# Layer 0's network: staged key weights scaled and stored behind the latest silu on ScalarE

## The chip, the core and the metric

The kernel runs on one core of one Trainium2 chip. The metric is the device time of one execution in microseconds (us). The core has five instruction queues that run side by side and wait for each other by semaphores: TensorE (PE in the profile; its weight loads are PEld), VectorE (DVE), ScalarE (ACT), GpSimd (POOL) and SyncE (SP), which computes nothing and issues most of the transfers. ACT and POOL issue some transfers as well. Each queue runs its instructions in the order in which they were put into it.

## The reference

The program is a two-layer decoder trunk for 512 tokens of width 1024. Layer 0 is a Mamba-2 mixer followed by a gated network with a width-3 causal convolution; layer 1 is differential attention, whose keys and values come from the stream after layer 0, followed by the same kind of network. What the change touches is the network of layer 0 and the key weights:

```python
def conv_ffn(x, ln_g, up_w, conv_w, conv_b, down_w):
    u = causal_dwconv(rms_norm(x, ln_g) @ up_w, conv_w, conv_b)
    gate, up = u[..., :FFN_DIM], u[..., FFN_DIM:]
    return (jax.nn.silu(gate) * up) @ down_w

def shared_kv(x, kv_ln_g, kv_w, k_norm_g):
    kv = rms_norm(x, kv_ln_g) @ kv_w          # first half of kv_w: the key weights
```

FFN_DIM is 2816, that is 22 blocks of 128 features. The gain `kv_ln_g` can be multiplied into the rows of `kv_w` ahead of time, and the kernel does so for the key half (1024x1024): it loads it, scales it row by row, and stores the scaled copy in a scratch tensor `ks` in DRAM, from which attention loads it later.

## The kernel before

Every product is made of three: each operand is split into a high part (rounded by an ACT copy) and a low part (the rest, by a DVE subtraction). For weights that means, for each chunk of 128x1024: a load on SP into a `wr_...` tile (three buffers), an ACT copy into `wh_...`, a DVE subtraction into `wl_...` (three buffers each), and then PE. `chunk()` lets ACT and DVE prepare two chunks ahead of the one that PE is about to use; a buffer comes free when PE is done with the chunk three places earlier.

PE's order is written out by hand in layer 0's network (`tc.manual_schedule`); on ACT, DVE and SP a scheduler sets the order from what the program issues, from its dependences and from its own estimate of when each will be ready. `with tc.issue_after(ins):` adds an order: what the block issues on the engine of `ins` stands behind `ins` there.

The network takes the 22 blocks in three parts (0 to 5, 6 to 13, 14 to 21). A plain block ("P") is two chunks, `h0_p_0` for the gate and `h0_p_1` for the up side. Blocks 8, 9 and 12, 13 are done in pairs ("S") by seven smaller products, in the order 5, 1, 2, 6, 7, 3, 4, with chunks `U0m_p`; plain chunks are mixed in between them. After its products, each block goes through the convolution (`taps`: one ACT copy at L1066, two DVE steps at L1068), the silu of the gate (L1478 for plain blocks, L1208 for pairs), the product of the two sides (L1160 on DVE), and a split into `sh`, `sl` (L1083 on ACT, L1084 on DVE), from which the down products take their input.

The staging is a side job in the same loop. `stage()` is called after each step and alternates: on one call `key_weights_in` loads an eighth of the key weights (512 KB) into the tile `stage` on SP (L1005), two calls later `key_weights_out` scales its two halves on ACT (L1011) and stores them to `ks`, issued from ACT too (L1012). There is one buffer: the load of the next eighth waits on SP until the store of this one has landed, and the scalings wait on ACT until the load has landed. Eight such rounds are made. The scheduler is free in where it puts them on ACT and SP, since nothing in layer 0 reads `ks`.

Of the kernel before, what the change touches and what calls it, by code (L numbers as in the profile page):

```python
# [12 lines left out]
AF = mybir.ActivationFunctionType  # L13
# [32 lines left out]
def trunk_kernel(ctx: ExitStack, tc, x, ssm_ln_g, ssm_in_w, ssm_conv_w, ssm_conv_b, ssm_dt_bias,  # L46
# [4 lines left out]
    act, dve, pool, pe, sync = nc.scalar, nc.vector, nc.gpsimd, nc.tensor, nc.sync  # L51
# [105 lines left out]
    state = {"next": 0, "use": 0, "hooks": {}}  # L157
# [842 lines left out]
    def key_weights(k0, i):  # L1000
        return ks[k0 * P:(k0 + 2) * P, i * 512:(i + 1) * 512].rearrange("(k p) c -> p k c", p=P)

    def key_weights_in(pl, n):
        v = pl.tile([P, 1024], F32, tag="stage", name="stage%d" % n, bufs=1).rearrange("p (k c) -> p k c", k=2)
        sync.dma_start(v, w_cols(kv_w, n // 2 * 2, 2, n % 2 * 512, 512)[0])  # L1005
        return n, v

    def key_weights_out(n, v):
        k0, i = n // 2 * 2, n % 2
        for k in range(2):  # L1010
            act.activation(v[:, k], v[:, k], AF.Copy, scale=c2[:, 32 + k0 + k:33 + k0 + k])  # L1011
        act.dma_start(key_weights(k0, i), v)  # L1012
# [19 lines left out]
    def ffn(l, norm, bp, gnext, nnext):  # L1032
        with (tc.tile_pool(name="ffn_h%d" % l, bufs=1) as hp, tc.tile_pool(name="ffn%d" % l, bufs=1) as fp,
# [23 lines left out]
            def taps(j, p, u):  # L1057
                key = "%s%d_%d" % ("gu"[j], l, p)
                if j:
                    v = bp.tile([P, T], F32, tag="nsq", name="v" + key, bufs=2)  # L1060
                elif l and vs[0] % 4 > 1:
                    v = bp.tile([P, T], F32, tag=("nacc", "nr")[vs[0] % 2], name="v" + key)
                else:
                    v = fp.tile([P, T], F32, tag="v", name="v" + key, bufs=2 if l else 4)
                vs[0] += 1 - j
                act.activation(v, u, AF.Identity, bias=tap_col(j, p, 3), scale=tap_col(j, p, 2))  # L1066
                for s in range(1, 3):
                    dve.scalar_tensor_tensor(out=v[:, s:], in0=u[:, :T - s], scalar=tap_col(j, p, 2 - s),  # L1068
                                             in1=v[:, s:], op0=ALU.mult, op1=ALU.add)
                return v  # L1070
# [404 lines left out]

            def tapped(p, us):
                ga = taps(0, p, us[0])
                act.activation(ga, ga, AF.Silu)  # L1478
                return ga, taps(1, p, us[1])

            staged = {"n": 0, "at": 0, "v": None}

            def stage():

                staged["at"] += 1
                if staged["v"] and staged["at"] > 1:
                    key_weights_out(*staged["v"])
                    staged.update(v=None, at=0)
                elif not staged["v"] and staged["n"] < KB and staged["at"] > 1:
                    staged.update(v=key_weights_in(fp, staged["n"]), n=staged["n"] + 1, at=0)  # L1490

            def plain(p, sides):

                pss = []
                for _ in whole(p, pss):
                    yield
                sides["open"] = p, tapped(p, pss)

            def gate(sides):
                p, (ga, up) = sides.pop("open")  # L1500
                gated(p, ga, up, sides)
                return ga
# [20 lines left out]
            for q in quarters[:2]:  # L1523
                split_whole(*q)
            gated(0, *tapped(0, (u0[:, 0], u0[:, 1])), sides)
            for q in quarters[2:]:
                split_whole(*q)
            u1 = evac(1, ps1)
            sums = chain(x_sums(0, *tmp[:2]), x_sums(2, *tmp[2:]))
            for p in range(2, 6):  # L1530
                for _ in plain(p, sides):
                    if p > 2:
                        next(sums, None)
                if p == 2:
                    gated(1, *tapped(1, (u1[:, 0], u1[:, 1])), sides)
                ga = gate(sides)
                next(sums, None)
                if p == 3:
                    down_ahead(*parts[0], "z")
                if not l and p == 3:  # L1540
                    bias_ranges(u_tile("ranges"), ga)
# [15 lines left out]
            for i in range(1, len(parts)):  # L1557
# [23 lines left out]
                for kind, p, step in order:  # L1581
                    if kind == "D":
                        q0, m = parts[i - 1]
                        down(q0, m, [behind[q0 + 2 * j] for j in range(m // 2)], False)
                        gate(sides)
                        continue
                    if p not in gens:
                        gens[p] = (plain if kind == "P" else double)(p, sides)
                    next(gens[p])
                    if kind == "P" and step == 1:  # L1590
                        run(gens[p])
                        if p > p0:
                            gate(sides)
                    if not l:
                        stage()
# [454 lines left out]
```

## Time and profile before

| what | value |
|---|---|
| median of 3 runs | 1314.4 us (1312.15 to 1316.61) |
| profiled execution, its own time | 1314.86 us |
| its span, first to last instruction | 1313.2 us |
| TensorE's mean granted clock | 0.999 |
| PE busy | 1304.0 us, 99% of the span |
| DVE, ACT, POOL busy | 1074.7, 748.0, 184.8 us |
| layer 0's network on PE | about 377 to 730 us of the span |
| scalings of staged key weights, L1011 | 16, first 360.6, last 433.2 us |

The span is read in microseconds from the first instruction. PE is almost always busy, so what counts is where it is not: the waits of PE, and stretches in which the granted clock (PEclk) is under 1.00. The busy shares of the other engines matter only where PE waits for one of them. A row of the timeline gives the start, the duration, the engine, the line, the operation with its output and inputs, and in brackets the idle time before it with what ended it.

### The profile page before, as it was taken

Reading aid. Unit: us, or ns where it says so; the run is one execution under the profiler, and the core shown is the slowest. Engines: PE = TensorE matmul, PEld = TensorE weight load, DVE = VectorE, ACT = ScalarE, POOL = GpSimd, SP = SyncE. Lnnn points to the kernel's source line nnn. Section 1 sums busy time; section 2 is a strip of 40 time slices with the busy share of each in tenths; the row PEclk is TensorE's granted clock in tenths of the full one; section 3 lists DMA queues with packets and bytes.
Section 4 is the critical chain, followed back from the end, with each engine's and each line's share of the span. In section 5 each row is a group of like instructions: output and inputs, shape, how many; then the busy total and the mean of one; then the engine's idle time right before and its main releaser. Section 6 shows DMA issues by size and latency. Waiting matters only on the chain.

```text
span 1313.2 us, 18936 instructions
## 1 busy us (share of the span) xinstructions
PE 1304.0 (99%) x7059; PEld 1106.4 (84%) x7059; DVE 1074.7 (82%) x1796; ACT 748.0 (57%) x1234; POOL 184.8 (14%) x212
## 2 busy tenths in 40 slices
PE   9999999999999999999999999999999999999998
PEld 8878888888888798999889887877888889988887
DVE  7989878889879876986768878677789977997776
ACT  6696554743367545653445667777656535643442
POOL 5230200300020421020002310000020030020001
PEclk9999999999999999999999999999999999999999
DMA  7553533432366797769337663222233586566325
GB/s 210 154 154 91 151 99 102 145 98 75 105 191 183 182 219 156 154 144 212 101 88 144 175 146 112 81 65 65 63 107 89 145 204 156 141 123 187 99 62 128
DMA packets 198588, 174.18 MB, mean 133 GB/s; under 512 B 7964, under 2 KB 172192, under 8 KB 198496
## 3 DMA queue, kind: packets, MB, share of 16 engines
q1 hardware_dynamic: 164336, 119.69, 30.9%
q0 software_dynamic: 30704, 47.99, 19.0%
q10 hardware_dynamic: 3456, 5.30, 1.2%
q8 instruction: 55, 0.90, 0.3%
q14 instruction: 37, 0.30, 0.1%
HBM read 166.51 MB, written 6.44 MB: 132 GB/s over the span
## 4 chain that ended last, share of the span: by engine, by line
PE 94%; DVE 2%; ACT 2%; DMA 1%; issue 0%; DVEq 0%; ACTq 0%; SPq 0%
PE ps_in L246 5%; PE ps_in L248 5%; PE ps_in L247 5%; PE ps_g L248 4%; PE ps_g L246 4%; PE ps_g L247 4%; PE ps_u L246 4%; PE ps_u L247 4%; PE ps_u L248 4%; PE ps_s L1439 3%; PE ps_s L1444 3%; PE ps_s L1442 3%; PE ps_s L1338 3%; PE ps_s L1341 3%; PE ps_s L1343 3%; PE ps_o L247 2%
## 5 line engine op out<-in xcount | busy, mean ns | idle before, releaser
L246 PE MATMUL ps_in<-xgh,wh_in 128*128 128x512 f32 x304 | 122.9, 404 | 0.0
L196 DVE TENSOR_TENSOR wl_h<-wr_h,wh_h 128x1024 fp32r<-128x1024 f32 x72 | 88.4, 1231 | 40.7 <-ACT wh_h L185 38.1
L248 PE MATMUL ps_in<-xgh,wl_in 128*128 128x512 f32 x304 | 119.7, 394 | 0.0
L247 PE MATMUL ps_in<-xgl,wh_in 128*128 128x512 f32 x304 | 119.2, 392 | 0.0
L248 PE MATMUL ps_g<-xgh,wl_h 128*128 128x512 f32 x288 | 112.9, 392 | 2.2 <-DVE wl_h L196 2.2
L247 PE MATMUL ps_g<-xgl,wh_h 128*128 128x512 f32 x288 | 112.7, 391 | 0.4 <-DVE xgl L1084 0.4
L246 PE MATMUL ps_g<-xgh,wh_h 128*128 128x512 f32 x288 | 113.0, 392 | 0.0
L246 PE MATMUL ps_u<-xgh,wh_h 128*128 128x512 f32 x288 | 112.1, 389 | 0.0
L247 PE MATMUL ps_u<-xgl,wh_h 128*128 128x512 f32 x288 | 112.1, 389 | 0.0
L248 PE MATMUL ps_u<-xgh,wl_h 128*128 128x512 f32 x288 | 112.1, 389 | 0.0
L185 ACT ACTIVATE wh_h<-wr_h 128x1024 fp32r<-128x1024 f32 x72 | 76.2, 1059 | 59.7 <-PE ps_u L247 17.2
L1083 ACT ACTIVATE sh<-vg 128x512 fp32r<-128x512 f32 (+1 forms) x81 | 42.2, 530 | 60.1 <-DVE vg L1160 35.1
L1238 POOL DMA_DIRECT2D wz<-in_ffn_down_w_dram x28 | 33.8, 1229 | 285.9 <-DVE wl_s L1277 125.2
L248 PEld LDWEIGHTS ps_in<-xgh,wl_in 128*128 128x128 f32 x304 | 57.1, 188 | 12.2 <-issue 0.4
L246 PEld LDWEIGHTS ps_in<-xgh,wh_in 128*128 128x128 f32 x304 | 57.2, 188 | 11.6 <-issue 1.3
L247 PEld LDWEIGHTS ps_in<-xgl,wh_in 128*128 128x128 f32 x304 | 57.3, 188 | 11.0 <-issue 0.5
L248 PEld LDWEIGHTS ps_g<-xgh,wl_h 128*128 128x128 f32 x288 | 54.5, 189 | 14.1 <-DVE wl_h L196 2.6
L247 PEld LDWEIGHTS ps_g<-xgl,wh_h 128*128 128x128 f32 x288 | 54.4, 189 | 11.8 <-DVE xgl L1084 0.8
L1444 PE MATMUL ps_s<-sl,wh_s 128*128 128x256 f32 x252 | 64.1, 283 | 0.0
L1442 PE MATMUL ps_s<-sh,wh_s 128*128 128x256 f32 x252 | 64.1, 283 | 0.0
L185 ACT ACTIVATE wh_in<-wr_in 128x1024 fp32r<-128x1024 f32 x39 | 41.2, 1057 | 39.8 <-PE ps_in L247 30.0
L1276 ACT ACTIVATE wh_s<-wz 128x1024 fp32r<-128x1024 f32 (+2 forms) x38 | 37.3, 981 | 46.7 <-PE ps_s L1343 16.5
(512 smaller groups left out, 3795.4 us busy)
## 6 DMA issues: line engine op xcount, KB each, us to landing
wr_h<-in_ffn_up_w_dram SPq DMA_DIRECT2D x60, 512.0 KB, 4.3
wr_in<-in_ssm_in_w_dram SPq DMA_DIRECT2D x40, 512.0 KB, 3.9
wz<-in_ffn_down_w_dram POOLq DMA_DIRECT2D x21, 512.0 KB, 5.8
m<-cumd POOLq DMA_DIRECT2D x16, 512.0 KB, 4.4
wr_out<-in_ssm_out_w_dram SPq DMA_DIRECT2D x16, 512.0 KB, 3.5
wr_s<-in_ffn_down_w_dram SPq DMA_DIRECT2D x13, 512.0 KB, 4.3
wr_h<-in_ffn_up_w_dram SPq DMA_DIRECT2D x24, 256.0 KB, 3.5
wx<-in_ffn_down_w_dram POOLq DMA_DIRECT2D x12, 512.0 KB, 7.2
```

The source lines that it names most:

```text
L185: return act.activation(self.wh[:, :self.n], self.raw[:, :self.n], AF.Copy)
L196: return eng.tensor_tensor(out=self.wl[:, :self.n], in0=self.raw[:, :self.n], in1=self.wh[:, :self.n].bitcast(F32), op=ALU.subtract)
L246: pe.matmul(ps, wh, xh, start=start, stop=False)
L247: pe.matmul(ps, wh, xl, start=False, stop=False)
L248: return pe.matmul(ps, wl, xh, start=False, stop=stop).ins
L1083: act.activation(hi, v, AF.Copy)
L1338: pe.matmul(pss[b], h, ws[q][1][:, cols], start=False, stop=end and q == qs[-1], skip_group_check=more)
L1341: pe.matmul(pss[b], h, ws[q][0][:, cols], start=first and q == qs[0], stop=False, skip_group_check=more)
L1343: pe.matmul(pss[b], w, ws[q][0][:, cols], start=False, stop=False, skip_group_check=more)
L1439: pe.matmul(v[:, b], wl[:, q, cols], h, start=False, stop=q == nq - 1, skip_group_check=not opens or b > 0)
L1442: pe.matmul(v[:, b], wh[:, q, cols], h, start=opens and q + b == 0, stop=False, skip_group_check=not opens or b > 0)
L1444: pe.matmul(v[:, b], wh[:, q, cols], w, start=False, stop=False, skip_group_check=not opens or b > 0)
```

## The change

The reference to the last silu instruction of a plain block is kept in `state["silu"]`, and the scalings and the store of a staged eighth are issued inside `tc.issue_after(state["silu"])`, that is, on ACT they stand behind the latest silu that the program has issued by then. The loads (L1005, on SP) have no such order of their own, nor has the last call after the loop. Nothing is added to or taken from the work.

```diff
             def tapped(p, us):
                 ga = taps(0, p, us[0])
-                act.activation(ga, ga, AF.Silu)
+                state["silu"] = act.activation(ga, ga, AF.Silu).ins
                 return ga, taps(1, p, us[1])
...
                 staged["at"] += 1
                 if staged["v"] and staged["at"] > 1:
-                    key_weights_out(*staged["v"])
+                    with tc.issue_after(state["silu"]):
+                        key_weights_out(*staged["v"])
                     staged.update(v=None, at=0)
```

The order of PE's and POOL's instructions is the same before and after. On ACT, DVE and SP it moves. In the names below the number at the end is that of the tile; the eight staged eighths are stage_4323, 4833, 4976, 5142, 5296, 5463, 6060 and 6225.

The first place is ACT where block 3 ends and blocks 4 and 5 begin, near 428 us of the profile. `vg_3` is the gate of block 3, `vg_4` that of block 4, `sh_3959` the split of blocks 2 and 3. Before:

```order
L185 ACTIVATE wh_h_5_1_4120<-wr_h_5_1_4118 128x1024
L1066 ACTIVATE vg_4_4150<-ps_g_4_4084,cf_90 128x512
L1011 ACTIVATE stage_6225<-stage_6225,c_89 128x512 x2
L1478 ACTIVATE vg_3_4034<-vg_3_4034 128x512
L1012 DMA ks<-stage_6225 128x2x512
L1083 ACTIVATE sh_3959<-vg_3_4034 128x512
```

With the change:

```order
L185 ACTIVATE wh_h_5_1_4120<-wr_h_5_1_4118 128x1024
L1066 ACTIVATE vg_4_4150<-ps_g_4_4084,cf_90 128x512
L1478 ACTIVATE vg_3_4034<-vg_3_4034 128x512
L1083 ACTIVATE sh_3959<-vg_3_4034 128x512
L185 ACTIVATE wh_h_6_0_4173<-wr_h_6_0_4171 128x1024
```

The eighth round, and with it all sixteen scalings, are gone from this part; the silu of block 3 no longer stands behind them.

The second place is ACT between the pairs 8, 9 and 12, 13, near 525 to 535 us of the profile. `u_8` holds the products of blocks 8 and 9, `wh_U_12_5054` and `wh_U_12_5113` are the high parts of the first two chunks of the pair 12, 13. Before:

```order
L185 ACTIVATE wh_h_11_0_5012<-wr_h_11_0_5010 128x1024
L1083 ACTIVATE sh_4969<-vg_10_4959 128x256
L1152 ACTIVATE wh_U_12_5054<-wz_0_3669 128x1024
L1066 ACTIVATE vg_8_5041<-u_8_4763,cf_90 128x512
L1083 ACTIVATE sh_4969<-vg_10_4959 128x256
L1066 ACTIVATE vg_9_5045<-u_8_4763,cf_90 128x512
```

With the change:

```order
L185 ACTIVATE wh_h_11_0_5012<-wr_h_11_0_5010 128x1024
L1011 ACTIVATE stage_5142<-stage_5142,c_89 128x512 x2
L1083 ACTIVATE sh_4969<-vg_10_4959 128x256
L1152 ACTIVATE wh_U_12_5054<-wz_0_3669 128x1024
L1012 DMA ks<-stage_5142 128x2x512
L1083 ACTIVATE sh_4969<-vg_10_4959 128x256
L1066 ACTIVATE vg_8_5041<-u_8_4763,cf_90 128x512
L1066 ACTIVATE vg_9_5045<-u_8_4763,cf_90 128x512
```

The fourth round now stands ahead of the first split of block 10 and of the pair's first chunk. Further up on ACT the first round stands behind the silu of block 7, the second ahead of `wh_h_10_1` and the third behind the silu of block 10; the fifth to eighth stand behind the silus of blocks 11, 14, 16 and 18.

The third place is SP, where the loads of the stage moved too. Before, all eight stood between the weights of blocks 0 to 6; the rows from block 10 on had none:

```order
L177 DMA wr_h_10_1_4865<-in_ffn_up_w_dram 128x8x128
L1143 DMA wr_U_8_4978<-in_ffn_up_w_dram 128x4x256
L177 DMA wr_h_11_0_5010<-in_ffn_up_w_dram 128x8x128
L177 DMA wr_h_11_1_5146<-in_ffn_up_w_dram 128x8x128
L1245 DMA wx_1_3672<-in_ffn_down_w_dram 128x4x256
L1245 DMA wx_0_3671<-in_ffn_down_w_dram 128x4x256
L1143 DMA wr_U_12_5178<-in_ffn_up_w_dram 128x4x256
```

With the change:

```order
L1143 DMA wr_U_8_4978<-in_ffn_up_w_dram 128x4x256
L1005 DMA stage_4833<-in_kv_w_dram 128x2x512
L177 DMA wr_h_11_0_5010<-in_ffn_up_w_dram 128x8x128
L1005 DMA stage_4976<-in_kv_w_dram 128x2x512
L177 DMA wr_h_11_1_5146<-in_ffn_up_w_dram 128x8x128
L1245 DMA wx_1_3672<-in_ffn_down_w_dram 128x4x256
L1245 DMA wx_0_3671<-in_ffn_down_w_dram 128x4x256
L1005 DMA stage_5142<-in_kv_w_dram 128x2x512
L1143 DMA wr_U_12_5178<-in_ffn_up_w_dram 128x4x256
```

The loads of the second, third and fourth eighth now stand between the weights of the pairs; the first is loaded where it was.

## The prediction

> **What bounds the kernel now.** I read the page first, then PE's waits, the windows around the staging, the timelines there and the chain of waits.
>
> ```profile
> PE 1304.0 (99%) x7059; PEld 1106.4 (84%) x7059; DVE 1074.7 (82%) x1796; ACT 748.0 (57%) x1234; POOL 184.8 (14%) x212
> ...
> PE ps_g L248 <- DVE wl_h L196: 2.2, 1, 2.2
> ...
> PE ps_g L247 <- DVE xgl L1084: 0.4, 1, 0.4
> ...
> 400.00:420.00 20.00, 19.59 (x87) 15.89 (x86) 18.91 (x28) 15.39 (x22) 0.20 (x1) 1.00 0.63 188
> 420.00:440.00 20.00, 17.79 (x73) 14.26 (x72) 17.92 (x30) 13.68 (x21) 3.75 (x3) 0.91 0.65 192
> ```
>
> PE is the bound: busy for 1304.0 of 1313.2 us. PE's order and work stay as they are, so the change can only move waits of PE, and of those the waits list shows two in layer 0's network, 2.2 and 0.4 us, both in the windows in which the stage is scaled (the columns of a window: its length, then PE, PEld, DVE, ACT and POOL busy, PEclk, DMA share, GB/s). In the second one PEclk is 0.91 too.
>
> PE's timeline tells what these waits cost:
>
> ```profile
> 406.95 0.39 PE L246 MATMUL ps_g<-xgh,wh_h 128*128 128x512 f32 x1
> 407.75 0.50 PE L247 MATMUL ps_g<-xgl,wh_h 128*128 128x512 f32 x1 [0.41 <-DVE xgl L1084]
> 408.08 0.39 PE L248 MATMUL ps_g<-xgh,wl_h 128*128 128x512 f32 x1
> ...
> 428.07 0.39 PE L246 MATMUL ps_u<-xgh,wh_h 128*128 128x512 f32 x1
> ...
> 433.51 0.39 PE L246 MATMUL ps_g<-xgh,wh_h 128*128 128x512 f32 x1
> 433.74 0.39 PE L247 MATMUL ps_g<-xgl,wh_h 128*128 128x512 f32 x1
> 436.33 0.79 PE L248 MATMUL ps_g<-xgh,wl_h 128*128 128x512 f32 x1 [2.21 <-DVE wl_h L196]
> 436.92 0.63 PE L246 MATMUL ps_g<-xgh,wh_h 128*128 128x512 f32 x1
> ...
> 439.99 0.39 PE L248 MATMUL ps_g<-xgh,wl_h 128*128 128x512 f32 x1
> ```
>
> Undisturbed, a chunk of 24 such matmuls takes 433.51 - 428.07 = 5.44 us, 0.227 each. From 433.74 to 439.99 stand ten steps, 2.27 us at that pace; they took 6.25. The wait of 2.21 therefore cost **3.98 us**: the wait, and some 1.8 us for matmuls at half pace behind it. The wait of 0.41 cost (407.75 - 406.95 - 0.23) + (0.33 - 0.23) = **0.67 us**, with no slow pace behind it.
>
> **Who is late there.** The chain of waits, and ACT's and DVE's timelines:
>
> ```profile
> 422.07 5.44 DMA ks<-stage
> ...
> 427.59 4.60 DMA stage<-in_kv_w_dram
> ...
> 432.56 1.34 ACT L1011 ACTIVATE stage<-stage,c 128x512 f32<-128x512 f32 x2 [2.79 <-DMA stage<-in_kv_w_dram]
> 433.80 0.61 ACT L1478 ACTIVATE vg<-vg 128x512 f32<-128x512 f32 x1
> ...
> 434.45 0.69 DVE L1160 TENSOR_TENSOR vg<-vg,vu 128x512 f32<-128x512 f32 x1 [2.08 <-ACT vg L1478]
> 435.06 1.22 DVE L196 TENSOR_TENSOR wl_h<-wr_h,wh_h 128x1024 fp32r<-128x1024 f32 x1
> ...
> 405.86 0.69 DVE L1160 TENSOR_TENSOR vg<-vg,vu 128x512 f32<-128x512 f32 x1 [1.09 <-ACT vg L1478]
> ...
> 412.68 0.69 DVE L1100 TENSOR_TENSOR wx<-wx 128x512 f32<-128x512 f32 x1
> 413.29 0.69 DVE L1101 TENSOR_TENSOR wz<-wz,wz 128x512 f32<-128x512 f32 x1
> ```
>
> The seventh store (5.44 us) lets SP load the eighth piece (4.60 us); ACT stands 2.79 us before its scalings, with block 3's silu behind them; DVE's product waits for that silu, and the low weights behind the product are what PE wants. At 405.86 the same thing in small: a silu behind a scaling held DVE for 1.09 us.
>
> **What the change removes.** With no scaling ahead of these silus, DVE loses the idle 1.09 and 2.08 us. The low weights that ended at 436.28 would end at 436.28 - 3.17 = 433.1, and at 432.5 with one step of the input's sums (L1100 on `wx`, 413.29 - 412.68 = 0.6) now behind them in DVE's order. PE wants them at 433.97, or at 433.3 with the earlier wait gone. So both PE waits go: 3.98 + 0.67 = **4.65 us** gained. The scalings' own 16 x 0.7 us were never on PE's path except there.
>
> **What it adds: the rounds in the new place.** A round is store, load, scaling, in that order, with one buffer. Its two transfers, by all eight of the trace:
>
> ```profile
> L1012 ACTq DMA_DIRECT2D ks<-stage x8: 366/366/406, 362.9 to 433.9; - x8
> ...
> DMA to landing us min/median/max: 2.8/3.8/5.4
> ...
> L1005 SPq DMA_DIRECT2D stage<-in_kv_w_dram x8: 367/368/368, 356.6 to 427.6; - x8
> ...
> DMA to landing us min/median/max: 3.9/4.6/5.0
> ```
>
> Round trip: median 3.8 + 4.6 = 8.4 us, at least 6.7, at most 10.4. The rounds two to four stand on ACT within 27 us of each other, and each scaling is on ACT in the way of what follows. ACT, DVE and PE at that place before:
>
> ```profile
> 499.28 0.63 ACT L1478 ACTIVATE vg<-vg 128x512 f32<-128x512 f32 x1 [2.13 <-DVE vg L1068]
> 500.37 1.06 ACT L185 ACTIVATE wh_h<-wr_h 128x1024 fp32r<-128x1024 f32 x1 [0.46 <-PE ps_u L247]
> ...
> 518.05 0.37 ACT L1195 ACTIVATE u<-ps_U 128x256 f32<-128x256 f32 x1
> ...
> 525.43 1.06 ACT L185 ACTIVATE wh_h<-wr_h 128x1024 fp32r<-128x1024 f32 x1 [0.89 <-PE ps_U L1187]
> 527.73 0.42 ACT L1083 ACTIVATE sh<-vg 128x256 fp32r<-128x256 f32 x1 [1.25 <-DVE vg L1160]
> ...
> 528.75 0.42 DVE L1084 TENSOR_TENSOR sl<-vg,sh 128x256 fp32r<-128x256 f32 x1
> ...
> 537.99 1.22 DVE L1153 TENSOR_TENSOR wl_U<-wz,wh_U 128x1024 fp32r<-128x1024 f32 x1
> ...
> 540.77 0.64 PE L1190 MATMUL ps_U<-xgh,wl_U 128*128 128x256 f32 x4
> ```
>
> In before's times (the gain shifts all of it alike): block 7's silu ends at 499.9. Round one: its piece has lain there since the start; two scalings (1.34) to 501.2, `wh_h_10_0` to 502.2, then the first store. Round two: piece lands at 502.2 + 8.4 = 510.6; two scalings with a split (0.5) between them, store at 512.4. Round three: lands at 520.8 (ACT is ready at 519.0, after the evacuation of 518.05 and block 10's silu); scaled and stored at 522.1. Round four: lands at 530.5, scaled by **531.9**. ACT gets to it at 526.5, behind `wh_h_11_0`, and stands for 4 us.
>
> Behind it on ACT is the split `sh` of 527.73, and on DVE everything that stood behind its `sl` of 528.75. That `sl` now starts 0.5 us after the scalings, at 532.4: 3.65 us late. DVE has no gap from there to the low weights at 537.99 (second chunk of the pair), so these end at 539.21 + 3.65 = 542.9. PE wants them at 540.77. New wait: 2.1 us, on PE. By the 2.21 above that costs 2.1 + 1.8 = **3.9 us**. The high part `wh_U_12_5054`, also behind the round, is done 1.4 us after the scalings, 533.3, ahead of PE's 536.9 (its chunk is the one before); the second's, now behind two silus, at about 539.6, ahead of DVE's turn.
>
> Bounds by the rows: with three round trips of 6.7 the fourth piece is scaled at 528.4 (ACT is ready for the third only at 519.0), `sl` is 0.15 late, less than the 1.56 in hand, and the new wait is nothing. With 10.4 each it is scaled at 537.9, `sl` is 9.7 late and the wait 8.1, with the slow pace 9.9 us. I take the medians: these three are near the middle of what each transfer showed. The window 512 to 532 has a higher DMA share (0.82) than 400 to 440:
>
> ```profile
> 512.00:532.00 20.00, 20.00 (x146) 18.95 (x145) 14.02 (x20) 11.23 (x17) 3.04 (x3) 1.00 0.82 196
> ```
>
> which speaks for longer rather than shorter trips.
>
> The other edits cost nothing that PE sees:
>
> ```profile
> 510.67 3.68 SPq L177 DMA_DIRECT2D wr_h<-in_ffn_up_w_dram  x2
> ...
> 536.91 1.06 ACT L185 ACTIVATE wh_h<-wr_h 128x1024 fp32r<-128x1024 f32 x1 [1.33 <-PE ps_g L247]
> ...
> 549.14 0.61 ACT L1478 ACTIVATE vg<-vg 128x512 f32<-128x512 f32 x1
> ```
>
> SP's weight loads now stand behind the stage's. `wr_h_11_1`, issued at 514, waits for the second store (512.4 + 3.8 = 516.2) and its fellow, so some 3 us; ACT wants it at 536.9. Round five is scaled behind the silu of 549.14, some 15 us after the fourth store, longer than any round trip, and the last three lie further apart; so no wait, and 1.34 us of ACT each. Their cover is ACT's idle time (it is busy for 11 of 20 us in the window above); without it each would be a late weight copy by 1.34 us.
>
> A rule on the slow pace: the Trainium skill, "TensorE: Matmul & The Clock Gate", part 1, has the clock fall after an idle window of about 3.4 us. Here it fell behind a wait of 2.21 (PEclk 0.91), so the measurement decides; by the rule alone the new wait would cost its 2.1 and nothing behind it, an estimate that lowers the sum by 1.8 us.
>
> **The sum.** Span 1313.2 - 4.65 + 3.9 = 1312.45; the execution's own time was 1.66 above its span, 1314.1; the median of the runs is 0.46 under that execution: **1313.6 us**.
>
> **Rivals.**
> *Fast trips (no new wait).* If the three trips total under about 23.5 us instead of 25.2, the wait is under 0.4 and the cost under 0.7. Then 1314.4 - 4.65 = 1309.8. For it: the shortest trips, 2.8 and 3.9, were in the same profile; against: three in a row, at the higher DMA share. The Trainium skill, "DMA: Bandwidth & Descriptors", section "Anatomy of one DMA", fits 2.0 us plus bytes over 436 GB/s on the gpsimd path: by that fit an estimate of 3.2 us for 512 KB, 6.4 for the pair, which would give this case; the trace does not agree, its medians are 3.8 and 4.6.
> *Slow trips.* From a new wait of 6.8 us on (cost 8.6) the kernel is measurably slower; the bound gives 9.9 - 4.65 = +5.25, 1319.6. For it: the trip of 5.44 + 4.60; against: it needs three of them.
> *DVE is the bound itself.* If DVE, 18.91 of 20 us busy, stays late at 433 without the stage, about half of the 4.65 is left: 1314.4 - 2.3 + 3.9 = 1316.0. Against it: DVE idled there, and for ACT alone.
> *No effect at all* is excluded: all sixteen scalings have moved, as ACT's order shows.
>
> **How the numbers follow.** Forecast 0.62, fast trips 0.18, slow trips 0.10, DVE-bound 0.10. A measurement of this kernel can tell 0.3%, 3.9 us: faster means under 1310.5, slower over 1318.3. Faster: 0.18 and 0.02 from the forecast's edge. Slower: 0.10 and 0.02. Same: 0.68. The range 1310.0 to 1317.5 leaves out about half of the fast case and the slow one; the forecast's own is 1311.5 to 1315.5.
>
> **What would show it.** Right: no PE wait at 407 and 434, PEclk 1.00 there; ACT waiting for `stage` around 522 and 526 to 531 (less the shift); one PE wait at L1190 of `ps_U` behind `wl_U`, about 2 us, with PEclk under 1.00 after it. Wrong: PE still waiting for `wl_h` in the first six blocks, no PE wait at all, or a PE wait after 560.

## The result, and the profile after

| | before | with the change |
|---|---|---|
| median (lowest to highest, runs) | 1312.64 us (1311.78 to 1316.61, 8) | 1318.16 us (1316.83 to 1319.06, 8) |
| ratio to before, 95% interval | | 1.0037 (1.0027 to 1.0048) |
| profiled execution, own time and span | 1314.86 and 1313.2 us | 1317.49 and 1315.8 us |

The change makes the kernel slower, by 0.3 to 0.4%: little, but clear of the noise. The median of before differs by two microseconds from one set of runs to the next (1314.56 of 14 and 1314.19 of 13 in the two sets of the experiments, against which 1318.16 is 0.27 to 0.30% more); the reason is looked for below. Between the two profiled executions, both of which hold a stretch of slow matmuls, the change costs 1315.8 - 1313.2 = 2.6 us.

PE's waits in the kernel with the change (engine, tile and line, what ended the wait, us in total, times, longest):

```profile
PE ps_U L1185 <- ACT wh_U L1152: 2.5, 1, 2.5
PE ps_U L1190 <- DVE wl_U L1153: 1.6, 1, 1.6
...
PE ps_U L1185 <- ACT u L1195: 0.3, 1, 0.3
```

The two waits of before, for `wl_h` and `xgl`, are gone, and the wait at L1190 of `ps_U` behind `wl_U` has come, with a longer one just ahead of it at L1185, behind the high part of the same weights. The windows say where the time went (length, then PE, PEld, DVE, ACT, POOL busy, PEclk, DMA share, GB/s):

```profile
400.00:420.00 20.00, 20.00 (x90) 16.54 (x89) 20.00 (x31) 13.08 (x19) 0.19 (x1) 1.00 0.20 59
420.00:440.00 20.00, 20.00 (x90) 16.57 (x89) 20.00 (x32) 10.31 (x16) 5.54 (x4) 1.00 0.67 159
500.00:520.00 20.00, 20.00 (x126) 18.08 (x125) 12.71 (x17) 12.57 (x20) 0.00 (x0) 1.00 0.71 220
520.00:540.00 20.00, 17.03 (x113) 15.46 (x111) 13.43 (x23) 11.50 (x19) 3.86 (x3) 0.96 0.98 227
540.00:560.00 20.00, 18.58 (x116) 17.38 (x117) 18.68 (x29) 13.11 (x22) 1.28 (x1) 0.87 0.61 161
```

From 400 to 440 PE is now busy without a gap and PEclk is 1.00, where it was 19.59 and 17.79 of 20 us, and 0.91. That DVE is busy for the whole of it, too, costs PE nothing. From 520 to 560 PE loses 2.97 and 1.42 us of busy time and the clock falls to 0.96 and 0.87. In 520 to 540 the DMA share is 0.98, where it was 0.79.

PE's timeline gives the sizes. Before:

```profile
536.93 0.28 PE L1185 MATMUL ps_U<-sEh,wh_U 128*128 128x256 f32 x1
...
542.69 0.40 PE L246 MATMUL ps_u<-xgh,wh_h 128*128 128x512 f32 x1
...
562.55 0.40 PE L246 MATMUL ps_g<-xgh,wh_h 128*128 128x512 f32 x1
```

With the change:

```profile
532.11 0.28 PE L1185 MATMUL ps_U<-sEh,wh_U 128*128 128x256 f32 x1
532.22 0.28 PE L1187 MATMUL ps_U<-sEl,wh_U 128*128 128x256 f32 x1
...
537.79 0.39 PE L1185 MATMUL ps_U<-xgh,wh_U 128*128 128x256 f32 x1 [2.48 <-ACT wh_U L1152]
...
538.88 0.41 PE L1185 MATMUL ps_U<-xgh,wh_U 128*128 128x256 f32 x1
539.10 0.41 PE L1187 MATMUL ps_U<-xgl,wh_U 128*128 128x256 f32 x1
541.09 1.22 PE L1190 MATMUL ps_U<-xgh,wl_U 128*128 128x256 f32 x4 [1.57 <-DVE wl_U L1153]
...
544.66 0.58 PE L246 MATMUL ps_u<-xgh,wh_h 128*128 128x512 f32 x1
...
565.29 0.40 PE L246 MATMUL ps_g<-xgh,wh_h 128*128 128x512 f32 x1
```

The rows are the start of the pair's first chunk, of the plain chunk behind its second, and of block 14. At the first PE is ahead by 536.93 - 532.11 = 4.82 us: the gain. At the next it is behind by 544.66 - 542.69 = 1.97: the pair's second chunk cost 6.8 us. At the last it is behind by 2.74, another 0.8. The second chunk's steps of 0.21 us (538.88 to 539.10), where 0.11 to 0.12 is the pace of the first (532.11 to 532.22), are the slow pace. Of the 6.8 us, 2.48 + 1.57 are waits; 2.4 are slow pace, since its 24 matmuls took 544.66 - 537.79 - 1.57 = 5.3 us without the wait inside them, and take 24 x 0.12 = 2.9 otherwise. The 0.3 us that are left are the pause around a wait that the profile does not count as idle.

What held the weights, on ACT and DVE:

```profile
506.20 0.72 ACT L1011 ACTIVATE stage<-stage,c 128x512 f32<-128x512 f32 x1 [3.49 <-DMA stage<-in_kv_w_dram]
...
516.01 1.34 ACT L1011 ACTIVATE stage<-stage,c 128x512 f32<-128x512 f32 x2 [1.34 <-DMA stage<-in_kv_w_dram]
...
528.90 1.34 ACT L1011 ACTIVATE stage<-stage,c 128x512 f32<-128x512 f32 x2 [7.24 <-DMA stage<-in_kv_w_dram]
...
530.58 0.43 DVE L1084 TENSOR_TENSOR sl<-vg,sh 128x256 fp32r<-128x256 f32 x1 [6.57 <-ACT sh L1083]
...
535.65 1.14 ACT L1208 ACTIVATE vg<-vg 128x512 f32<-128x512 f32 x2
536.69 1.04 ACT L1152 ACTIVATE wh_U<-wz 128x1024 fp32r<-128x1024 f32 x1
...
539.82 1.21 DVE L1153 TENSOR_TENSOR wl_U<-wz,wh_U 128x1024 fp32r<-128x1024 f32 x1
```

ACT stands for 7.24 us before the fourth eighth's scalings. DVE stands for 6.57 us with it, for the split behind them, and from there DVE has no gap up to the pair's second low part (539.82), and ACT one of 0.47 us up to its high part (536.69). PE is waiting for both. The chain of waits shows the three round trips (start, length, what; store, then load):

```profile
495.89 5.22 DMA ks<-stage
501.13 4.98 DMA stage<-in_kv_w_dram
508.09 3.61 DMA ks<-stage
511.76 4.16 DMA stage<-in_kv_w_dram
517.38 4.77 DMA ks<-stage
522.23 6.59 DMA stage<-in_kv_w_dram
```

10.2, 7.8 and 11.4 us: 29.5 in sum, where the sum of the prediction had 25.2.

### The profile page after: what moved, and what is told of

Its sections match the earlier page's. It is cut to its first block, busy times and chain, and to the rows that moved or that the text cites. A ratio compares the mean times of both kernels' runs of the same rounds, so it can differ in the third digit from the quotient of the medians.

```text
span 1315.8 us, 18951 instructions
## 1 busy us (share of the span) xinstructions
PE 1304.8 (99%) x7059; PEld 1107.8 (84%) x7059; DVE 1075.4 (82%) x1796; ACT 747.0 (57%) x1234; POOL 185.2 (14%) x212
## 4 chain that ended last, share of the span: by engine, by line
PE 93%; DVE 2%; DMA 2%; ACT 2%; issue 1%; DVEq 0%; ACTq 0%; SPq 0%
PE ps_in L246 5%; PE ps_in L248 5%; PE ps_in L247 5%; PE ps_u L246 5%; PE ps_g L246 5%; PE ps_g L247 5%; PE ps_u L247 5%; PE ps_g L248 5%; PE ps_u L248 5%; PE ps_s L1439 3%; PE ps_s L1444 3%; PE ps_s L1442 3%; PE ps_s L1338 3%; PE ps_s L1341 3%; PE ps_s L1343 3%; PE ps_o L247 2%
## 5 line engine op out<-in xcount | busy, mean ns | idle before, releaser
L247 PEld LDWEIGHTS ps_u<-xgl,wh_h 128*128 128x128 f32 x288 | 54.2, 188 | 11.2
L248 PEld LDWEIGHTS ps_u<-xgh,wl_h 128*128 128x128 f32 x288 | 54.1, 188 | 11.3
```

The source lines that it names most:

```text
L247: pe.matmul(ps, wh, xl, start=False, stop=False)
L248: return pe.matmul(ps, wl, xh, start=False, stop=stop).ins
```

## The experiments

Two questions were open. Is the fourth round's lateness the whole of the loss, and is what made it late the round trips? And why do the times of before lie up to 5 us apart?

**The fourth round behind a later silu.** The changed kernel, in which the fourth eighth alone stands behind the silu of the pair 8, 9 (L1208), some 7 us of work further down ACT's queue, and the others where the change has them:

```diff
-                            act.activation(ga[b], ga[b], AF.Silu)
+                            state["pair"] = act.activation(ga[b], ga[b], AF.Silu).ins
...
-                    with tc.issue_after(state["silu"]):
+                    with tc.issue_after(state["pair" if staged["v"][0] == 3 else "silu"]):
```

> The change with one difference: the scalings and the store of the fourth piece stand behind the silus of blocks 8 and 9 (L1208), all other rounds as in the change. Theory (the fourth round, late by three serial round trips, stands in front of the pair 12, 13 on ScalarE): both PE waits for the pair's second chunk go, 6.8 us less than the change, about 1311.4 us. Rival (the loss is the extra ScalarE work and the new order among the pairs, or weight loads late behind the stage's loads on SyncE): all of that is still there, so within 1.5 us of the change, 1316.5 to 1318.5.

Measured: 1310.98 us (1310.66 to 1312.19, 7 runs), ratio to before 0.9974 (0.9963 to 0.9985); span 1309.3. ACT's rows of the staging in this kernel:

```profile
516.05 1.34 ACT L1011 ACTIVATE stage<-stage,c 128x512 f32<-128x512 f32 x2 [2.31 <-DMA stage<-in_kv_w_dram]
...
530.50 1.32 ACT L1011 ACTIVATE stage<-stage,c 128x512 f32<-128x512 f32 x2
```

The fourth scalings run later than with the change (530.50 for 528.90) and no engine stands for them, since ACT has other work ahead of them now. Both waits near 537 and 541 are gone, and with them 1318.16 - 1310.98 = 7.2 us of the median, 6.5 of the span. Rounds one to three stand where the change put them, so the loss was the place of the fourth. (The scheduler also moved the pair's second high part ahead of the silus of blocks 8 and 9; the next experiment leaves it behind them.) One wait stays:

```profile
PE ps_U L1185 <- ACT u L1195: 1.5, 1, 1.5
```

It is the 0.3 us wait of the changed kernel, grown, at 550. The fifth round alone does not make it: the kernel of the third experiment has that round in the same place, and no such wait. But here ACT also stood 1.52 and 1.68 us for weights of the pair (`wz`, near 539 and 543), which the other kernel, with no fourth round in this part, does not show. Whether the moved fourth round is behind that is not shown.

**One store less between the third round and the fourth.** The changed kernel without the third store; the fourth eighth is stored twice instead, so that the count of transfers stays:

```diff
-        act.dma_start(key_weights(k0, i), v)
+        if n != 2:
+            act.dma_start(key_weights(k0, i), v)
+        if n == 3:
+            act.dma_start(key_weights(2, 0), v)
```

> The change without the third piece's store: its place in the scratch tensor gets a second store of the fourth piece instead, so a quarter of a half of the key weights is wrong and the output with it; the work is the same otherwise. The fourth load then waits for the third scalings alone and not for a store. Theory (serial round trips make the fourth round late): the fourth scalings come 4 to 5 us earlier, the PE waits of 2.5 and 1.6 us shrink to under 1 us together, 5 to 6.5 us less than the change, 1311.5 to 1313. Rival (ScalarE work and order): 1317 to 1318.5, with PE waits as in the change.

Measured: 1311.19 us (1310.04 to 1311.46, 6 runs), ratio 0.9973 (0.9962 to 0.9984). The fourth scalings:

```profile
523.23 1.34 ACT L1011 ACTIVATE stage<-stage,c 128x512 f32<-128x512 f32 x2 [2.90 <-DMA stage<-in_kv_w_dram]
524.48 1.04 ACT L185 ACTIVATE wh_h<-wr_h 128x1024 fp32r<-128x1024 f32 x1
```

With the store of about 4.8 us out of the chain, the fourth eighth is scaled 5.7 us earlier, ACT stands for 2.9 instead of 7.24 us, and PE's only wait at the pair is 0.5 us for `wl_U`. The order on ACT is nearly the one of the change: the scheduler put the fourth scalings one instruction earlier, ahead of `wh_h_11_0` (524.48) instead of behind it, and everything behind them as far as the pair's second chunk stands as it did. So with the fourth round still in front of the pair, a shorter chain of round trips takes the loss away: it is their length that costs the time, not the order itself.

**Only the last four rounds behind the silu.** The first four are left to the scheduler:

```diff
-                    with tc.issue_after(state["silu"]):
+                    with tc.issue_after(state["silu"]) if staged["v"][0] > 3 else nullcontext():
```

> The change for the last four rounds only; the first four are left where the scheduler puts them, as before. Theory: no round is left in 400 to 434 and none in front of the pair 12, 13, so neither the wait at 434 nor those of the change are there; a small wait of 0.3 us behind the fifth round may stay: about 1310 to 1311 us, under both kernels. Rival (any scaling among the pairs and the last plain blocks costs PE time): above 1313.

Measured: 1310.42 us (1309.68 to 1310.8, 6 runs), ratio 0.9968 (0.9956 to 0.998). It is the lowest median of all, under before and under the change. PE's windows in this kernel:

```profile
420.00:440.00 20.00, 20.00 (x90) 16.57 (x89) 20.00 (x32) 11.13 (x16) 5.34 (x4) 1.00 0.66 160
500.00:520.00 20.00, 20.00 (x126) 18.08 (x125) 12.69 (x17) 10.05 (x15) 2.02 (x2) 1.00 0.49 139
520.00:540.00 20.00, 20.00 (x139) 18.71 (x139) 19.94 (x34) 14.79 (x25) 3.13 (x3) 1.00 0.79 145
```

The gain in 420 to 440 stays, and with no round between 490 and 540 the DMA share there is 0.49 and 0.79 in place of 0.71 and 0.98, and the list shows no wait of PE in layer 0's network. So the gain of the change comes with the last four rounds being away from 407 and 434, and moving rounds one to four added only loss.

**Why the fourth load was long.** It took 6.59 us, beyond the 5.0 that was the most before. At 520.0, 2 us ahead of it, GpSimd issues two transfers that accumulate into `wx`, and at 523.0 SyncE two of the pair's weights. This run takes the accumulations out of that part and leaves the orders of ACT and SP as they are:

```diff
-                if k == "z" and not l:
+                if k == "z" and not l and p0 != PARTS_D[1][0]:
```

> The changed kernel without the two transfers of GpSimd into `wx` (the accumulations at L1238, issued near 520 and 8.6 us in flight in its trace), so half of one part's summed down weights is missing; the orders of ScalarE and SyncE stay. Why did the fourth piece's load take 6.6 us? Theory: because it shared the transfer engines with these and with the pair's weights. Then the load takes 5.0 us or less, the fourth piece is scaled at least 1.5 us earlier, the two waits of PE near 537 and 541 sum to 2.5 us or less instead of 4.1, and the time falls by 1.5 to 4 us against the changed kernel, to 1314 to 1316.5. Rival: the load is long through its own queue (the weights of the pair issued beside it on SyncE) and the accumulations do not matter; then it takes 6 us or more again, the waits are about 4 us, and the time is within 1 us of 1318.

Measured: 1315.56 us (1313.18 to 1317.05, 10 runs), ratio 1.0011 (1.0002 to 1.0021), 2.6 us under the change's median and 1.9 under the run of the change that stands beside it below. Its chain of waits, and then its ACT and PE rows:

```profile
517.53 4.64 DMA ks<-stage
522.26 4.36 DMA stage<-in_kv_w_dram
```

```profile
526.70 1.34 ACT L1011 ACTIVATE stage<-stage,c 128x512 f32<-128x512 f32 x2 [5.42 <-DMA stage<-in_kv_w_dram]
...
535.59 0.39 PE L1185 MATMUL ps_U<-xgh,wh_U 128*128 128x256 f32 x1 [0.83 <-ACT wh_U L1152]
...
538.89 0.74 PE L1190 MATMUL ps_U<-xgh,wl_U 128*128 128x256 f32 x4 [2.08 <-DVE wl_U L1153]
```

The load is issued at the same moment (522.26) behind the same store and takes 4.36 us. The scalings come 2.2 us earlier, and so does the low part (PE goes on at 538.89, not 541.09). DVE's order is the same as well. So the long load is shown to come from the accumulations beside it (through what they get in each other's way is not); the pair's weights, still there, do not make it long without them. The kernel of the first experiment agrees: there the same load, issued at 522.48 beside the accumulations, took 7.0 us, and cost nothing, since nothing stood for it. PEclk is 1.00 from 520 to 560 in this profile, so the slow pace is missing from its span of 1312.3 us, too. Of its ten runs three have the mean clock of 0.997 that all eight runs of the change have, so a part of the 2.6 us is the slow pace coming less often. The waits sum to 2.91 us, a little over the 2.5 expected: the three trips still take 10.3 + 8.1 + 9.1 = 27.5 us.

**Does it come again?** A second profile of the kernel with the change, as it is:

> The changed kernel, unchanged. Theory: the waits near 537 and 541 come again, 3.5 to 4.5 us in sum, with a trip of over 10 us for the fourth piece, since the same transfers meet at the same place in every execution; half pace behind them costs 1.5 to 2 us or nothing. Rival: the long load of 6.6 us was chance of one execution; then the trip is 9 us or less, the waits sum to 2.5 us or less, and the time is under 1316.5.

Measured: 1317.42 us, waits of 2.2 and 2.0 us, and from its chain:

```profile
511.76 4.24 DMA stage<-in_kv_w_dram
...
517.45 4.72 DMA ks<-stage
522.26 6.18 DMA stage<-in_kv_w_dram
```

4.72 + 6.18 us and the gap between them make 11.0. The long trip came again, in the same place: it was no chance of one execution.

**The spread of before.** Two more profiles of the kernel before:

> The kernel before once more, for a second look at its own PE waits. If the wait of 2.2 us for the low weights near 434 us (and the 0.4 us near 407) belongs to the kernel, it stands again at the same place with the half-pace matmuls behind it, 3.5 to 4.5 us in all. If it hung on one slow store and load of the staged weights in that one execution, it is under 1 us here and the span is 2 us or more shorter (about 1311 instead of 1313.2).

> The kernel before, unchanged. In one profile the matmuls behind PE's wait of 2.2 us ran at half pace (1.8 us), in a second they did not behind a wait of 2.06 us. Theory: whether the slow pace comes differs from execution to execution, and with it the time, so an execution near 1314.5 shows it (PEclk under 0.95 in 420 to 440) and one near 1312 does not. Rival: the slow pace has no part in the spread of this kernel's times; then the two do not go together here.

Measured: 1312.1 us in the first, 1314.56 in the second. PE's rows, of the first:

```profile
435.17 0.50 PE L248 MATMUL ps_g<-xgh,wl_h 128*128 128x512 f32 x1 [2.06 <-DVE wl_h L196]
435.51 0.40 PE L246 MATMUL ps_g<-xgh,wh_h 128*128 128x512 f32 x1
435.75 0.40 PE L247 MATMUL ps_g<-xgl,wh_h 128*128 128x512 f32 x1
```

And of the second:

```profile
436.03 0.61 PE L248 MATMUL ps_g<-xgh,wl_h 128*128 128x512 f32 x1 [2.08 <-DVE wl_h L196]
436.44 0.63 PE L246 MATMUL ps_g<-xgh,wh_h 128*128 128x512 f32 x1
436.87 0.63 PE L247 MATMUL ps_g<-xgl,wh_h 128*128 128x512 f32 x1
```

The wait is the same to 0.02 us, so it belongs to the kernel; the half pace that was expected with it came in the second alone. In the first the matmuls behind it come every 0.24 us and PEclk is 1.00 from 420 to 440; in the second they come every 0.43 and PEclk is 0.91, as in the profile that the prediction read. The slow pace comes in some executions and not in others, and the time goes with it. The mean clock of each run goes the same way: of the 27 runs of before that stand beside the experiments, the six with a clock of 1.000 all took under 1314 us and the four with 0.997 or 0.998 over 1314.9; the other 17, with 0.999, lie on both sides. That it makes the whole spread is not shown, only the 1.6 to 1.8 us of it that these rows hold.

## Why the prediction was wrong

*What bounds the kernel, and what the change removes: right.* PE's two waits went, the slow pace of 420 to 440 went, and PE is 4.82 us ahead at the pair, where 4.65 was worked out. In one of the later profiles of before the same wait carried no slow pace, so the gain is 4.65 in one execution and about 3 in another; the prediction had the former as a constant.

*DVE as the bound itself: refuted.* DVE is busy for 40.00 of the 40 us from 400 to 440, and PE does not wait for it.

*What it adds: right in mechanism, wrong in size.* The fourth round stands where it was put, ACT and DVE wait for it, and `wl_U` of the pair's second chunk is late at L1190. The step that failed is the term **"I take the medians"**, a round trip of 8.4 us, three times. They took 29.5 us and not 25.2: the first 1.8 us over the median, the second 0.6 under it, the third 3.0 over it. Set against that, the first store went out at 495.89, 1.5 us ahead of the forecast 502.2 less the gain of 4.8; the scalings between added 0.3. So the fourth eighth was scaled by 530.24 and not by 531.9 - 4.8 = 527.1: 3.1 us late. The prediction's own working then gives the rest: the low part 3 us later than 542.9 - 4.8 = 538.1, measured 541.0; PE's matmuls at 541.09, which is 5.1 behind the 540.77 - 4.82 = 535.95 at which it would have wanted them, forecast 2.1 + 3; and 1.7 us of slow pace behind, forecast 1.8. The term is 6.8 us instead of 3.9. That a part of the 5.1 shows as a wait for the high part is the same lateness: the prediction had that part "behind two silus, at about 539.6", and it came 3 us after that, too.

*Why the medians were the wrong row.* The eight transfers of each kind had been read where the staging stood before, at a DMA share of 0.62 to 0.69 (the windows from 360 to 440). The row of 512 to 532 with its 0.82 was quoted, and said to speak for longer trips, but it moved no number. Nor did it hold the moved transfers themselves: with them the share from 520 to 540 is 0.98. And the upper bound of a trip, 10.4, was broken by the third one (11.4), because its load met the accumulations into `wx`, which had not stood beside any of the eight. The run without them shows this term alone: 4.36 us for 6.59, and up to 2.6 us of the median. The first trip was long again in the kernels without these accumulations (10.3) and with the later fourth round (9.9); what makes it long no run tested.

*The Trainium skill on the two disputed prices.* By the Trainium skill, "DMA: Bandwidth & Descriptors", section "Anatomy of one DMA", a transfer of this size would take 3.2 us, an estimate by its fit, which it gives for transfers issued by GpSimd; the trace does not agree, the three loads of the stage here, issued by SyncE, took 4.2 to 6.6 us. By the Trainium skill, "TensorE: Matmul & The Clock Gate", part 1, the clock falls after at least one idle window of about 3.4 us; here it fell behind a wait of 2.48 with the change, and behind 2.08 but not behind 2.06 before. The measurement decides: a wait under that length can bring the slow pace.

*The other edits: nearly right.* The late `wr_h_11_1` cost nothing, and ACT did not wait for rounds five to eight. But PE lost another 0.8 us up to block 14, 0.3 of it in a wait for an ACT copy behind the fifth round. Another 0.2 are the end of the slow pace (0.42 from 544.66 to the next start, where 0.23 is the pace). Whether the round is the cause of the wait is open: without a fourth round ahead of it, it stands in the same place and PE does not wait.

*The sum.* By spans 1313.2 - 4.8 + 6.8 + 0.8 = 1316.0, measured 1315.8; forecast 1312.45. From the span to the median the forecast subtracted 0.46 from the execution's own time, since that was how before stood; with the change the profiled execution was 0.67 under the median, another 1.1 us. And the sum took from a profile with the slow pace a gain that the runs without it do not have.

*The rivals and the chances.* "Slow trips" was given 0.10 because "it needs three of them". It needed two: the second trip, 7.8 us, was even under the median. Nor were they draws from the eight: the third came out long in each of three profiles with the accumulations beside it. The measurement lies between that rival and the forecast. The cases treated the trips as symmetric about the median, when the one row that bore on them spoke for one side.

## What to carry to other kernels

A side job that is moved brings its own transfers with it: price its round trips at the traffic of the new place plus its own, with the other queues' transfers at that minute, not at the medians of the old place. On an engine that runs in order, an instruction that waits for a transfer holds everything behind it on that engine and on the engines it feeds (here 7.24 us on ACT and 6.57 on DVE), so what matters is how far apart such instructions stand against the longest trip, not the middle one; putting one of them some 7 us further down, or leaving the first four rounds where they had been, turned a loss of some 4 us into a gain of some 4. Where a stall has a step in its price (here the slow pace, some 1.6 to 2.4 us), one profile does not tell which side of the step the median is on.

## What the runs showed of the hardware that was not expected

The slow pace of TensorE behind a wait is not a function of the wait's length alone: 2.06 us brought none, 2.08 us, in the same place of the same program, some 3 us of matmuls at 0.43 instead of 0.24 us each. Nor does it begin with the wait. In the second profile of the changed kernel the matmuls behind the first wait still ran at full pace, and those behind the second at half; but the windows show that the clock had fallen ahead of the second wait:

```profile
537.41 0.39 PE L1185 MATMUL ps_U<-xgh,wh_U 128*128 128x256 f32 x1 [2.20 <-ACT wh_U L1152]
...
540.71 1.22 PE L1190 MATMUL ps_U<-xgh,wl_U 128*128 128x256 f32 x4 [2.04 <-DVE wl_U L1153]
```

```profile
538.00:539.00 1.00, 0.67 (x6) 0.42 (x4) 1.00 (x3) 1.00 (x3) 0.00 (x0) 0.72 1.13 301
...
545.00:546.00 1.00, 1.00 (x5) 0.77 (x5) 1.00 (x4) 0.44 (x3) 0.00 (x0) 0.87 1.25 201
```

With the clock at 0.5 when it is down, the PEclk of 0.72 in the first window puts the fall at 538.44, a microsecond behind the end of the first wait (537.41), and the 0.87 in the last puts its end at 545.26: 6.82 us. The first profile of the change gives 6.84 us by the same working (PEclk 0.61 and 0.97 in these two windows). In before it lasted 3.42 and 3.40 us (0.57 and 0.72, and 0.64 and 0.66, in 436 to 437 and 439 to 440), half as long. So the clock moves in steps of some 3.4 us.

The clock records in the traces are finer and say why 2.06 and 2.08 us can differ. In all nine traces the stretches between two changes of the clock, from its first rise on, are whole multiples of 3.413 us, so these steps are laid out by the start of the execution and not by the wait. Where the clock fell inside layer 0's network, the step that ended there held 2.0 us or more of the wait (2.01, 2.08, 2.20, 2.48). In the profile with 2.06 us a step ends at 434.43, in the middle of the wait (433.11 to 435.17), and neither step holds more than 1.32 us of it; without the accumulations the wait of 2.08 us is cut too, and its larger part is 1.83 us. This fits every profile here, but no run varied it by itself.

And a load of 512 KB into one buffer, issued within 0.03 us of the same moment behind the same store, took 6.59 and 6.18 us with two accumulating transfers in flight beside it and 4.36 without them.
